# Split steps of a gate's weights respaced, the last norm factor's transfers on GpSimd's queue, and an activation table loaded at another place

## The chip, the cores and the metric

The kernel runs on 1 core of a Trainium2 chip. The metric is the device time of one execution in microseconds. The core's engines are TensorE (PE), VectorE (DVE), ScalarE (ACT), GpSimd (POOL) and SyncE (SP, which here only issues DMAs). They run apart from each other, each through its own instructions in order, and wait for one another by semaphores.

## The reference

One encoder layer on 1024 tokens of width 1024 (float32). Cut to what matters here:

```python
u = x @ w_in                                   # rq, rk, rv, rg, aq, ak, av
y_ret = bidirectional_retention(rq, rk, rv)    # 8 heads, chunks of 128
y_ret = group_norm(y_ret) * gn_gain * silu(rg) # (y - mu) * rsqrt(var + eps)
y_att = windowed_gqa(aq, ak, av, sink)         # 8 query heads, 2 kv heads
mix = concat(y_ret, y_att) @ w_out
h = layer_norm(alpha * x + mix)
ffn = (silu(h @ w_ffn_gate) * (h @ w_ffn_up)) @ w_ffn_down
ple = p @ w_ple_proj
h = layer_norm(alpha * h + ffn + sigmoid(h @ w_ple_gate) * ple)
```

## The kernel before

The order of every engine is that in which the kernel's Python calls its operations (a manual schedule). The large products run on TensorE in three passes (lines L77 to L79 and L803 to L805): each float32 operand is split into a rounded part and the rest, by a copy on ScalarE (L71) and a subtraction on VectorE (L72), and the passes are high by high, high by low and low by high. Many of the products are also put together in Strassen's manner, from seven block products instead of eight.

The layer goes by stages. First come the mixers: four pairs of heads (NPAIR = 4), each with its projections, retention and attention. Then the product with w_out, the first norm, the product of the per-layer gate (w_ple_gate, with a sigmoid), the gate and up products of the feed-forward part (the units of the list gunits, with silu), the product down, and the second norm.

Retention of a pair: `bt<-rv,qq` and `bt<-rv,pt` are TensorE's products L428, whose right sides qq and pt VectorE makes at L411; L490 and L491 do the like for the pair before. The norm of a pair's y is taken in two halves, hh = 0 and 1. TensorE sums the squares, VectorE makes a row of variances (L500), and then five steps follow, put off by the ticks of LAGS: `spread` (L505, the row into a tile sn of 128 x 8 by way of DMAs), `power` (L508, the power -1/2 on GpSimd), `store` (L511, sn into rnd in DRAM, 4 KB), `fetch` (L515, two DMAs that bring rnd back into a tile spread over 64 partitions each, 128 KB each; the tile is called kv for hh = 0 and rb for hh = 1), and `scaled` (L519, y times the gain times that tile, on VectorE). The last pair's second half (self.i = 3, hh = 1) is the last factor that the product with w_out waits for.

Beside the mixers' own work runs what later stages need, given as a list of (tick, step) pairs. `presplit_gate` makes the blocks of the per-layer gate's weights: for each of four k it loads two blocks of 512 KB (L653, at the times of load(k)) and then does seven steps. A step adds up to one sum on VectorE (L663, or none) and one `put`: a copy on ScalarE (L602), a subtraction on VectorE (L603, out<-in names pro<-pre,pro) and a store of 512 KB on SP (L604, pgd<-pro). The steps use two tiles pro in turn, so a step's copy waits for the store of the step before the last. The tick of each step is in the list `at`; one tick is a little over a microsecond of the mixers' time. With load(3) and an empty step there are 30 entries.

An instruction on ScalarE may need an activation table that is not loaded. A table load is then placed ahead of it (ACT_TABLE_LOAD). The tiny activation at L1854 has no other use than to have silu's table loaded; L1388 is the first silu that computes something, L1097 are the sigmoids, and L1424 and L1426 bring results of the units out of PSUM.

Of the kernel before, what the change touches and what calls it, by code (L numbers as in the profile page):

```python
# [11 lines left out]
AF = mybir.ActivationFunctionType  # L12
# [10 lines left out]
NPAIR = 4  # L23
# [19 lines left out]
def layer(tc, xT, xn, w_first, w_mt, w_rv, w_out, w_pg, w_pe, pT, w_gu, w_dn,  # L43
          consts, dec_b, dec_c, sink, gng, lnp, out):
    nc = tc.nc
    act, dve, pool, pe, sp = nc.scalar, nc.vector, nc.gpsimd, nc.tensor, nc.sync
# [12 lines left out]
    def nm(s):  # L59
        uid[0] += 1  # L60
        return f"{s}{uid[0]}"
# [19 lines left out]
    def behind(ins):  # L81

        tc.add_manual_dep(ins.ins, recent[0], mybir.DependencyInfo(
            mybir.DependencyClass.NoSync, mybir.DependencyReason.DATA), reason="order")
        return ins
# [35 lines left out]
    def a_tile(shape, name, tag=None, dt=F32):  # L121

        turnA[0] += tag is None
        return big.tile(list(shape), dt, tag=tag or f"A{turnA[0] % 2}", bufs=4, name=nm(name))
# [8 lines left out]
    def bt(shape, tag, bufs=None, dt=F32):  # L133
        return bpool.tile(list(shape), dt, tag=tag, bufs=bufs, name=nm(tag))
# [15 lines left out]
    with tc.manual_schedule(engines={mybir.EngineType.DVE, mybir.EngineType.SP}):  # L150
        for kt in range(KT):
            r = xraw[kt]
# [240 lines left out]
    class Retention:  # L393
# [100 lines left out]
        def norm(self, hh):  # L494

            b = self.o.rearrange("p n c -> p (n c)")
            for k in range(2):
                pe.matmul(b, ones, self.sq[k], start=k == 0, stop=k == 1)
            row = bt([2, HF], "kv0")
            behind(dve.tensor_scalar(row, b[0:2], 1.0 / 64, EPS, ALU.mult, ALU.add))  # L500
            sm, r, home = bt([P, 2, 8], "sn", 1), bt([P, HF], ("kv1", "rb")[hh]), rnd[2 * self.i + hh]

            def spread():
                for h in range(2):
                    sp.dma_start(sm[64 * h:64 * h + 64, 0], row[h:h + 1].rearrange("o (q e) -> o q e", e=8))  # L505

            def power():
                behind(pool.tensor_tensor(sm[:, 1], sm[:, 0], cst[:, C_MH:C_MH + 1].to_broadcast([P, 8]), ALU.pow))  # L508

            def store():  # L510
                sp.dma_start(home, sm[:, 1])  # L511

            def fetch():
                for h in range(2):
                    sp.dma_start(r[64 * h:64 * h + 64], home[64 * h:64 * h + 64].rearrange("q e -> (q e)").partition_broadcast(64))  # L515

            def scaled():
                y = self.half(hh)
                behind(dve.scalar_tensor_tensor(y, y, gn[:, self.i:self.i + 1], r, ALU.mult, ALU.mult))  # L519

            later.extend((ticks[0] + at, f) for at, f in zip(LAGS, (spread, power, store, fetch, scaled)))
# [79 lines left out]
    def put(x, o, dst):  # L601
        behind(act.activation(o[:, 0, :], x, AF.Copy))  # L602
        behind(dve.tensor_tensor(o[:, 1, :], x, o[:, 0, :].bitcast(F32), ALU.subtract))  # L603
        sp.dma_start(dst, o.bitcast(F32))  # L604
# [40 lines left out]
    def presplit_gate():  # L645

        first, other = ([a_tile([P, 2, HF], "pre", t) for _ in range(2)] for t in ("A1", "A0"))
        ops = [a_tile([P, 2, HF], "pro", "A1", F32R) for _ in range(2)]
        n = [0]

        def load(k):
            for j in range(2):
                sp.dma_start((other if k == 1 else first)[j], w_pg[j, k])  # L653

        def steps(k):
            raw = other if k == 1 else first

            (a11, a21), (a12, a22) = ([raw[j][:, i, :] for i in range(2)] for j in range(2))

            def s(p, x, *sums):  # L660
                def f():
                    for a in sums:
                        behind(dve.tensor_tensor(*a))  # L663
                    put(x, ops[n[0] % 2], pgd[p - 1, k])
                    n[0] += 1
                return f

            return [s(1, a11), s(4, a22), s(2, a12), s(5, a22, (a22, a21, a22, ALU.add)),
                    s(7, a21, (a21, a11, a21, ALU.subtract)), s(6, a11, (a11, a22, a11, ALU.subtract)),
                    s(3, a12, (a12, a12, a11, ALU.subtract))]  # L670

        load(0)
        load(1)
        k0, k1, k2, k3 = map(steps, range(4))
        k1[0] = pair_of(k1[0], lambda: load(2))
        k3[0:0] = [lambda: load(3), lambda: None]
        at = [2 + 3.4 * k for k in range(12)] + [55 + 2.5 * k for k in range(2)] + [65 + 1.9 * k for k in range(7)] + \
            [78.5 + 2 * k for k in range(9)]
        return [(ticks[0] + t, f) for t, f in zip(at, k0 + k1 + k2 + k3, strict=True)]

    def pair_of(f, g):
        def both():
            f()
            g()
        return both
# [4 lines left out]
    def ytile(k):  # L690
        if ys[k] is None:
            ys[k] = a_tile([P, S], "y", "A0" if k < 4 else "A1")
        return ys[k]
# [46 lines left out]
    with tc.manual_schedule(engines={mybir.EngineType.PE}):  # L740
# [17 lines left out]
        r = Retention(0, y0, states)  # L758
# [6 lines left out]
        for i in range(1, NPAIR):  # L765
            assert i == 1 or not side, len(side)
            r = Retention(i, ytile(2 * i), states)
# [419 lines left out]
    frights, fsum = {}, []  # L1187
# [305 lines left out]
    for n in range(NP):  # L1493
        for u in plan(n):
            k = len(gunits)
# [51 lines left out]
    def op_arena(t, n=4):  # L1547
        arena("op", t, n)
# [249 lines left out]
    def ahead_g(k, upto):  # L1798

        def finish():  # L1800
            while urgent:
                urgent.pop(0)()

        units = [g[3] for g in gunits] + [2.72]
        room = units[k + 1] - gunits[k][4] - debt[0] if k >= 0 else 100.0
        while items and items[0].unit < upto and items[0].slots <= len(oslots) and (items[0].us <= room or items[0].unit <= k + 1):
            room -= items[0].us
            items.pop(0).issue()
            finish()
        finish()  # L1810
        if held and held[0][0].unit <= k + 1:
            release()
        debt[0] = max(-0.6, -room)
# [25 lines left out]
    with tc.manual_schedule(engines={ET.PE, ET.DVE, ET.Activation, ET.Pool, ET.SP}):  # L1839
        for _ in range(4):  # L1840
            oslots.append(wp.tile([P, 2, HF], F32R, tag="w", bufs=4, name=nm("w")))
            oslots.append(ct([P, 2, HF], "u", 4, F32R))
        sums2.extend(a_tile([P, 2, HF], "sums") for _ in range(2))
        fa = big16((P, 4, 2, 2, Q))
        halves4 = [(fa[:, k, 0], fa[:, k, 1]) for k in range(4)]
        halves4.append(tuple(ct([P, 2, Q], "sg", 2, F32R) for _ in range(2)))
        fsum.extend([cst[:, 0:Q], cst[:, Q:2 * Q], *(ct([P, Q], "fs", 2) for _ in range(2))])
        fwide = ct([P, 2, Q], "p", 2)
        fine, more = fine_right(2, halves4[:3]), fine_right(4, halves4[3:])
        fine += more  # L1850
        homes.update((name, a_tile([P, 2, HF], "ev")) for name in ("spare", "s1", "u2", "c11", "u3", "c22"))
        FINE4 = len(plan(0)) + len(plan(1)) - 2
        FINES = (2, 4, 7, 9, 20, 23, 26, FINE4)
        act.activation(fsum[3][:, 0:1], fsum[0][:, 0:1], AF.Silu)  # L1854
        ahead_g(-1, 4)
        for k in range(NG):
            gunits[k][1]()
            gunits[k][2]()
            if k in FINES:
                at = max([-1] + [i for i, x in enumerate(items) if x.right]) + 1  # L1860
                for x in fine.pop(0):
                    at += 1
                    x.unit, x.right = items[at].unit, True
                    items.insert(at, x)
                    at += 1
            ahead_g(k, k + 1 + min(9, 4 + k))
            while stores and stores[0][0] <= k:
                stores.pop(0)[1]()
            j = k + 1 - NG
            if j == -6:  # L1870
                while items:
                    items.pop(0).issue()
                release()
                arenas_a()
                op_arena(ct([P, 4, 2, HF], "h0a", dt=F32R))
                arena("chain", ct([P, 8, HF], "h0b"), 8)
            if j == -4:
                for _ in range(3):
                    op_arena(big16((P, 4, 2, HF)))
            if j >= -6:  # L1880
                ahead(0, j + 7)
            if j >= -4:
                ahead(1, j + 5)
        arena("b", big.tile([P, 8, HF], F32, tag="H", bufs=4, name=nm("H")), 8)
        arena("chain", ct([P, 8, HF], "h2"), 8)
        op_arena(ct([P, 4, 2, HF], "h3", dt=F32R), 4)
        rings["op"] += [ct([P, 2, HF], "u", 4, F32R) for _ in range(2)]
        for k in range(ND):
            d_step(k)
# [83 lines left out]
```

## Time and profile before

| | us |
|---|---|
| median of 3 runs | 1171.9 |
| lowest, highest run | 1169.49, 1171.92 |
| the profiled execution's own time | 1172.7 |
| its span in the trace | 1170.6 |
| TensorE busy in it | 1156.5 |
| VectorE, ScalarE, GpSimd busy | 900.4, 580.1, 121.0 |

Times in the trace count from the span's start. A row of a timeline has the start, the duration, the engine, the line, the operation and its tiles, and in square brackets the idle time before it and what ended that. A row of a table of waits has the engine and its line, what it waited for, the sum of the waits, their number and the longest. A row of the DMA view has the destination and source, the issuing queue, the number, the size of one and the median time from issue to landing. The granted clock of TensorE was 0.998 of full speed.

### The profile page before, as it was taken

What the parts mean: (1) busy time and instruction counts of PE and PEld (TensorE: products, weight loads), DVE (VectorE), ACT (ScalarE), POOL (GpSimd) and SP (SyncE); (2) the same over time, 40 slices, a digit from 0 to 9 for tenths busy, and PEclk for the clock granted to TensorE, in tenths of its full rate; (3) what the DMA queues carried; (4) which work ended last, traced back from release to release, by engine and by line L of the source; (5) the groups of instructions that cost most, each with busy time, mean ns of one, the idle gap of its engine ahead of it and who ended that gap; (6) DMA issues with size and microseconds to landing.
All of it is one profiled execution on the core that took longest, in us unless ns stands there. A gap on an engine that the chain in (4) does not pass through costs nothing.

```text
span 1170.6 us, 17933 instructions
## 1 busy us (share of the span) xinstructions
PE 1156.5 (99%) x6330; PEld 971.5 (83%) x6330; DVE 900.4 (77%) x1746; ACT 580.1 (50%) x1181; POOL 121.0 (10%) x181
## 2 busy tenths in 40 slices
PE   9999999999999999999999999999999999999996
PEld 7888888788887888888888888888888888888885
DVE  4666688777869688947998988888888976773677
ACT  5566348686756256214445434443344445552463
POOL 2001021202010021000000000000000020133232
PEclk9999999999999999999999999999999999999999
DMA  6345665746356955665322222232223289999977
GB/s 252 100 153 207 246 207 193 244 159 223 127 190 230 365 172 196 261 195 201 117 90 105 112 105 100 102 135 101 99 72 136 89 249 349 350 225 203 261 173 216
DMA packets 84378, 213.86 MB, mean 183 GB/s; under 512 B 12225, under 2 KB 17473, under 8 KB 84289
## 3 DMA queue, kind: packets, MB, share of 16 engines
q1 hardware_dynamic: 75648, 195.94, 47.6%
q0 software_dynamic: 8640, 16.78, 8.2%
q8 instruction: 50, 0.82, 0.3%
q14 instruction: 40, 0.32, 0.1%
HBM read 141.32 MB, written 62.16 MB: 174 GB/s over the span
## 4 chain that ended last, share of the span: by engine, by line
PE 86%; DVE 6%; DMA 4%; ACT 2%; issue 1%; POOL 0%; SPq 0%; DVEq 0%; ACTq 0%; POOLq 0%
PE bmm L803 8%; PE bmm L804 8%; PE bmm L805 7%; PE bt L803 6%; PE bt L804 6%; PE bt L805 6%; PE bmm L77 4%; PE bs L803 4%; PE bs L805 4%; PE bs L804 4%; PE bmm L79 4%; PE bmm L78 4%; PE bo L805 3%; PE bo L803 3%; PE bo L804 3%
## 5 line engine op out<-in xcount | busy, mean ns | idle before, releaser
L77 PE MATMUL bmm<-H,w 128*128 128x512 f32 x240 | 97.3, 405 | 0.0
L78 PE MATMUL bmm<-H,w 128*128 128x512 f32 x240 | 93.9, 391 | 0.0
L79 PE MATMUL bmm<-H,w 128*128 128x512 f32 x240 | 93.9, 391 | 0.0
L1388 ACT ACTIVATE ev<-ev 128x512 f32<-128x512 f32 x42 | 26.5, 630 | 104.3 <-DVE ev L1417 92.8
L1562 POOL DMA_DIRECT2D h0b<-in_w_dn x24 | 21.6, 899 | 540.7 <-DVE ev L1368 504.9
L77 PEld LDWEIGHTS bmm<-H,w 128*128 128x128 f32 x240 | 45.1, 188 | 11.1 <-issue 1.4
L79 PEld LDWEIGHTS bmm<-H,w 128*128 128x128 f32 x240 | 45.1, 188 | 10.3
L78 PEld LDWEIGHTS bmm<-H,w 128*128 128x128 f32 x240 | 45.2, 188 | 7.9
L554 ACT ACTIVATE sc<-sc,st 128x385 f32<-128x385 f32 (+1 forms) x64 | 37.2, 585 | 15.6 <-DVE st L552 15.3
L550 DVE CUSTOM_DVE_ANT_0 sc<-cst,bs,skb 128x384 f32<-128x384 f32 (+1 forms) x64 | 35.0, 575 | 8.3 <-PE bs L549 7.8
L1417 DVE TENSOR_TENSOR ev<-ev,bt 128x512 f32<-128x512 f32 x44 | 30.1, 683 | 12.5 <-PE bt L805 12.5
L1368 DVE TENSOR_TENSOR ev<-ev,bs 128x256 f32<-128x256 f32 x63 | 25.6, 418 | 15.5 <-PE bs L805 14.7
L1390 DVE TENSOR_TENSOR ev<-ev 128x512 f32<-128x512 f32 x42 | 29.0, 691 | 10.5 <-ACT ev L1388 9.0
L803 PE MATMUL bmm<-H,u 128*128 128x512 f32 x92 | 36.2, 393 | 0.2 <-ACT ev L1426 0.2
L804 PE MATMUL bmm<-H,u 128*128 128x512 f32 x92 | 36.0, 392 | 0.0
L805 PE MATMUL bmm<-H,u 128*128 128x512 f32 x92 | 35.8, 389 | 0.0
L72 DVE TENSOR_TENSOR w<-raw,w 128x512 fp32r<-128x512 f32 x34 | 23.1, 688 | 16.2 <-ACT w L71 16.1
L545 POOL COPY sc<-skb 128x1 f32<-128x1 f32 x64 | 15.6, 253 | 188.9 <-PE bt L572 144.5
L560 ACT ACTIVATE sc<-sc,st 128x384 f32<-128x384 f32 (+1 forms) x64 | 34.2, 580 | 1.2 <-DVE st L558 0.9
L71 ACT ACTIVATE H<-ln 128x512 fp32r<-128x512 f32 (+1 forms) x34 | 22.7, 675 | 21.2 <-DVE ln L1052 7.2
L803 PE MATMUL bmm<-H,w 128*128 128x512 f32 x84 | 32.9, 392 | 0.0
L804 PE MATMUL bmm<-H,w 128*128 128x512 f32 x84 | 32.9, 392 | 0.0
(802 smaller groups left out, 3898.4 us busy)
## 6 DMA issues: line engine op xcount, KB each, us to landing
ad<-ev SPq DMA_DIRECT2D x33, 512.0 KB, 2.6
pgd<-pro SPq DMA_DIRECT2D x28, 512.0 KB, 3.0
raw<-in_w_gu SPq DMA_DIRECT2D x22, 512.0 KB, 3.6
ln<-in_w_gu SPq DMA_DIRECT2D x22, 512.0 KB, 3.9
raw<-ad SPq DMA_DIRECT2D x40, 256.0 KB, 5.6
ln<-ad SPq DMA_DIRECT2D x37, 256.0 KB, 6.0
H<-in_w_dn SPq DMA_DIRECT2D x33, 256.0 KB, 7.4
wod<-aq SPq DMA_DIRECT2D x15, 512.0 KB, 2.8
```

The costliest lines, as they stand in the source:

```text
L77: pe.matmul(o, lh, rh, start=start, stop=False)
L78: pe.matmul(o, lh, rl, start=False, stop=False)
L79: recent[0] = pe.matmul(o, ll, rh, start=False, stop=stop).ins.name
L550: dve.tensor_tensor_reduce(sc[g][:, :nk], cst[:, tc0:tc0 + nk], b[:, :nk], slope(i, g), skb[:, 2 * i + g:2 * i + g + 1], ALU.add, ALU.max, ...
L554: act.activation(sc[g][:, :nk + 1], sc[g][:, :nk + 1], AF.Exp, bias=st_[:, 1, j, g:g + 1], accum_out=st_[:, 2, j, g:g + 1])
L560: behind(act.activation(sc[g][:, :nk], sc[g][:, :nk], AF.Copy, scale=st_[:, 3, j, g:g + 1]))
L803: pe.matmul(o, lh, rh, start=start, stop=False, skip_group_check=True)
L804: pe.matmul(o, lh, rl, start=False, stop=False, skip_group_check=True)
L805: pe.matmul(o, ll, rh, start=False, stop=stop, skip_group_check=True)
L1388: act.activation(c[:, 0, :], c[:, 0, :], AF.Silu)
L1390: dve.tensor_tensor(c[:, 1, :], c[:, 0, :], c[:, 1, :], ALU.mult)
L1417: dve.tensor_tensor(get(name), ev[left][:, m, :], right, ALU.add)
```

## The change

Three things are changed. In `presplit_gate` the list of ticks is spread otherwise: 14 entries from tick 2 in steps of 2.8, then 7 from tick 60 and 9 from tick 73 in steps of 1.9. Before there were 12 from tick 2 in steps of 3.4, 2 from 55, 7 from 65 and 9 from 78.5. In `norm` the store and the fetch of the last pair's second half are issued by GpSimd (pool) in place of SP. And the tiny silu activation is called behind the first unit of the gate in place of ahead of all units.

```diff
--- before.py
+++ after.py
@@ -500,6 +500,8 @@
             behind(dve.tensor_scalar(row, b[0:2], 1.0 / 64, EPS, ALU.mult, ALU.add))
             sm, r, home = bt([P, 2, 8], "sn", 1), bt([P, HF], ("kv1", "rb")[hh]), rnd[2 * self.i + hh]
 
+            q = pool if hh and self.i == NPAIR - 1 else sp
+
             def spread():
                 for h in range(2):
                     sp.dma_start(sm[64 * h:64 * h + 64, 0], row[h:h + 1].rearrange("o (q e) -> o q e", e=8))
@@ -508,11 +510,11 @@
                 behind(pool.tensor_tensor(sm[:, 1], sm[:, 0], cst[:, C_MH:C_MH + 1].to_broadcast([P, 8]), ALU.pow))
 
             def store():
-                sp.dma_start(home, sm[:, 1])
+                q.dma_start(home, sm[:, 1])
 
             def fetch():
                 for h in range(2):
-                    sp.dma_start(r[64 * h:64 * h + 64], home[64 * h:64 * h + 64].rearrange("q e -> (q e)").partition_broadcast(64))
+                    q.dma_start(r[64 * h:64 * h + 64], home[64 * h:64 * h + 64].rearrange("q e -> (q e)").partition_broadcast(64))
 
             def scaled():
                 y = self.half(hh)
@@ -674,8 +676,7 @@
         k0, k1, k2, k3 = map(steps, range(4))
         k1[0] = pair_of(k1[0], lambda: load(2))
         k3[0:0] = [lambda: load(3), lambda: None]
-        at = [2 + 3.4 * k for k in range(12)] + [55 + 2.5 * k for k in range(2)] + [65 + 1.9 * k for k in range(7)] + \
-            [78.5 + 2 * k for k in range(9)]
+        at = [2 + 2.8 * k for k in range(14)] + [60 + 1.9 * k for k in range(7)] + [73 + 1.9 * k for k in range(9)]
         return [(ticks[0] + t, f) for t, f in zip(at, k0 + k1 + k2 + k3, strict=True)]
 
     def pair_of(f, g):
@@ -1851,7 +1852,6 @@
         homes.update((name, a_tile([P, 2, HF], "ev")) for name in ("spare", "s1", "u2", "c11", "u3", "c22"))
         FINE4 = len(plan(0)) + len(plan(1)) - 2
         FINES = (2, 4, 7, 9, 20, 23, 26, FINE4)
-        act.activation(fsum[3][:, 0:1], fsum[0][:, 0:1], AF.Silu)
         ahead_g(-1, 4)
         for k in range(NG):
             gunits[k][1]()
@@ -1864,6 +1864,8 @@
                     items.insert(at, x)
                     at += 1
             ahead_g(k, k + 1 + min(9, 4 + k))
+            if k == 0:
+                act.activation(fsum[3][:, 0:1], fsum[0][:, 0:1], AF.Silu)
             while stores and stores[0][0] <= k:
                 stores.pop(0)[1]()
             j = k + 1 - NG
```

TensorE's order is the same in both. The lines of after are two higher than those of before from L503 on, one higher from L679 to L1853, and again two from L1867 on. The numbers in the names below are those of buffers.

VectorE, from the last split steps of pair 1's stage up to pair 2's pt; pre and pro are the gate's blocks. Before:

```order
L603 TENSOR_TENSOR pro_1168<-pre_1163,pro_1168 128x512
L663 TENSOR_TENSOR pre_1164<-pre_1164,pre_1163 128x512
L519 SCALAR_TENSOR_TENSOR y_1596<-y_1596,gn,kv_2110 128x512
L251 SCALAR_TENSOR_TENSOR aq_2236<-bmm_2242,aq_2236 64x512
L411 TENSOR_TENSOR qq_2330<-bt_2325,kd 128x512
L603 TENSOR_TENSOR pro_1167<-pre_1163,pro_1167 128x512
L251 SCALAR_TENSOR_TENSOR aq_2237<-bmm_2242,aq_2237 64x512
L411 TENSOR_TENSOR qq_2330<-bt_2325,kd 128x512
L603 TENSOR_TENSOR pro_1168<-pre_1164,pro_1168 128x512
L72 TENSOR_TENSOR w_2335<-raw_2333,w_2335 128x512
L72 TENSOR_TENSOR w_2338<-raw_2333,w_2338 128x512
L411 TENSOR_TENSOR pt_2360<-bt_2355,kd 128x512 x2
```

After:

```order
L665 TENSOR_TENSOR pre_1164<-pre_1164,pre_1163 128x512
L251 SCALAR_TENSOR_TENSOR aq_2249<-bmm_2125,aq_2249 64x512
L605 TENSOR_TENSOR pro_1168<-pre_1164,pro_1168 128x512
L500 TENSOR_SCALAR kv_2288<-bo_2201 2x512
L72 TENSOR_TENSOR w_2335<-raw_2333,w_2335 128x512
L521 SCALAR_TENSOR_TENSOR y_1604<-y_1604,gn,kv_2116 128x512
L411 TENSOR_TENSOR qq_2330<-bt_2325,kd 128x512
L251 SCALAR_TENSOR_TENSOR aq_2248<-bmm_2254,aq_2248 64x512
L411 TENSOR_TENSOR qq_2330<-bt_2325,kd 128x512
L72 TENSOR_TENSOR w_2338<-raw_2333,w_2338 128x512
L251 SCALAR_TENSOR_TENSOR aq_2249<-bmm_2254,aq_2249 64x512
L411 TENSOR_TENSOR pt_2360<-bt_2355,kd 128x512 x2
```

In before two L603 and two L72 stand between the first qq (L411) and pt, and L663 and L603 right up to the norm L519. In after all the L605 and L665 (before's L603 and L663) lie ahead of L521 (before's L519), and the last of them ahead of L500.

SP's queue at the last factor; sn is the factor as made on GpSimd, u and w are loads for the product with w_out. Before:

```order
L604 DMA ped<-aq_3046 128x1024
L505 DMA sn_3719<-kv_3717 64x1x8 x2
L511 DMA rnd<-sn_3719 128x8
L604 DMA ped<-aq_3046 128x1024
L515 DMA rb_3720<-rnd 64x512 x2
L814 DMA u_3835<-wod 128x1024
L814 DMA w_3837<-wod 128x1024
L814 DMA u_3839<-wod 128x1024
```

After:

```order
L606 DMA ped<-aq_3046 128x1024
L507 DMA sn_3719<-kv_3717 64x1x8 x2
L606 DMA ped<-aq_3046 128x1024
L815 DMA u_3835<-wod 128x1024
L815 DMA w_3837<-wod 128x1024
L815 DMA u_3839<-wod 128x1024
```

GpSimd's queue at the same place, after:

```order
L547 COPY sc_3606<-skb 128x1
L510 TENSOR_TENSOR sn_3564<-sn_3564,cst 128x8
L510 TENSOR_TENSOR sn_3719<-sn_3719,cst 128x8
L513 DMA rnd<-sn_3719 128x8
L517 DMA rb_3720<-rnd 64x512 x2
L915 TENSOR_TENSOR stt_3930<-stt_3930,cst 128x1
```

VectorE behind it, where L519 (L521 in after) takes the factor and H are splits for the product with w_out. Before:

```order
L723 SCALAR_TENSOR_TENSOR sq_3788<-sq_3788,bmm_3761 128x512
L724 SCALAR_TENSOR_TENSOR y_2323<-sq_3788,y_2323 128x512
L519 SCALAR_TENSOR_TENSOR y_2323<-y_2323,gn,rb_3720 128x512
L72 TENSOR_TENSOR H_3849<-y_1162,H_3849 128x512
L72 TENSOR_TENSOR H_3849<-y_468,H_3849 128x512
L72 TENSOR_TENSOR H_3849<-y_1596,H_3849 128x512
```

After:

```order
L605 TENSOR_TENSOR aq_3046<-rk_3047,aq_3046 128x512
L724 SCALAR_TENSOR_TENSOR sq_3788<-sq_3788,bmm_3761 128x512
L725 SCALAR_TENSOR_TENSOR y_2323<-sq_3788,y_2323 128x512
L72 TENSOR_TENSOR H_3849<-y_1162,H_3849 128x512
L521 SCALAR_TENSOR_TENSOR y_2323<-y_2323,gn,rb_3720 128x512
L72 TENSOR_TENSOR H_3849<-y_468,H_3849 128x512
```

The store and the two fetches have left SP's queue and stand on GpSimd's behind the power, and the first split H ahead of the scaling by the factor.

ScalarE at the first gate unit. Before:

```order
L1097 ACTIVATE sg_5328<-H_4563 128x512
L1424 ACTIVATE ev_5354<-bmm_5368 128x512
L1252 ACTIVATE w_5342<-sums_5346 128x512
L1424 ACTIVATE ev_5354<-bmm_5386 128x512
L1252 ACTIVATE u_5343<-sums_5347 128x512
L1388 ACT_TABLE_LOAD
L1388 ACTIVATE ev_5358<-ev_5358 128x512
```

After:

```order
L1098 ACTIVATE sg_5328<-H_4563 128x512
L1425 ACTIVATE ev_5354<-bmm_5367 128x512
L1253 ACTIVATE w_5342<-sums_5346 128x512
L1868 ACT_TABLE_LOAD
L1868 ACTIVATE fs_5352<-cst 128x1
L1425 ACTIVATE ev_5354<-bmm_5386 128x512
L1253 ACTIVATE u_5343<-sums_5347 128x512
```

The table load stands two operations earlier, ahead of the second eviction L1425 (before's L1424). The load that before makes at L1854, in the product with w_out, is not in after's order.

## The prediction

> **What bounds the kernel now.** I read the busy shares first, then TensorE's waits, then the timelines around the few waits that the change touches.
>
> ```profile
> PE 1156.5 (99%) x6330; PEld 971.5 (83%) x6330; DVE 900.4 (77%) x1746; ACT 580.1 (50%) x1181; POOL 121.0 (10%) x181
> PE bt L428 <- DVE pt L411: 2.0, 1, 2.0
> PE bo L142 <- POOL sq L139: 1.3, 1, 1.3
> PE bs L803 <- ACT h0b L972: 0.6, 1, 0.6
> PE bt L803 <- DMA u<-wod: 0.4, 1, 0.4
> PE bt L77 <- DMA p<-ptd: 0.3, 1, 0.3
> PE bt L572 <- ACT ptr L574: 0.3, 1, 0.3
> PE bmm L803 <- ACT ev L1426: 0.2, 1, 0.2
> ```
>
> TensorE is busy 1156.5 of 1170.6 us and all that it waits for by the profile comes to about 5 us. TensorE's order does not change, so no more than these waits can be gained, and whatever is made late elsewhere must appear here as a new one. The largest, 2.0 us, lies where retention pair 1 gives way to pair 2. What is won or lost before the end of the mixers stays won or lost: TensorE has no idle time afterwards in which to catch up.
>
> **Part 1, the split steps.** VectorE ahead of that wait, and TensorE at it:
>
> ```profile
> 216.80 0.98 DVE L491 TENSOR_TENSOR rb<-qq,pt 128x512 fp32r<-128x512 f32 x1
> ...
> 219.13 0.69 DVE L663 TENSOR_TENSOR pre<-pre,pre 128x512 f32<-128x512 f32 x1
> ...
> 223.59 0.69 DVE L603 TENSOR_TENSOR pro<-pre,pro 128x512 fp32r<-128x512 f32 x1 [0.40 <-ACT pro L602]
> 224.19 0.68 DVE L663 TENSOR_TENSOR pre<-pre,pre 128x512 f32<-128x512 f32 x1
> ...
> 228.92 0.68 DVE L603 TENSOR_TENSOR pro<-pre,pro 128x512 fp32r<-128x512 f32 x1
> ...
> 230.73 1.28 DVE L411 TENSOR_TENSOR pt<-bt,kd 128x512 f32<-128x512 f32 x2
> 229.16 1.03 PE L428 MATMUL bt<-rv,qq 128*64 128x64 f32 x28
> 232.16 1.04 PE L428 MATMUL bt<-rv,pt 128*64 128x64 f32 x28 [1.97 <-DVE pt L411]
> ```
>
> From L491 to the two pt of L411, VectorE has one gap, 0.40 us: it is simply full. In that stretch the order of before has 21 operations, that of after 15. The six that have gone are three L603 and three L663 of the gate's splits. Their starts follow one another by about 0.61 us (223.59 to 224.19), so pt comes some 3.6 us earlier, and TensorE needs it only 2.0 us earlier (229.16 + 1.03 for the first L428, so 230.2 in place of 232.16). The surplus of 1.6 us is the cover if something else there is late. Take −2.0. Bounds: 0 if another input holds pt, and no better than −2.0, since the first L428 runs straight on from TensorE's earlier work.
>
> The steps that leave go earlier, and two more of them fall in pair 0's stage:
>
> ```profile
> 168.62 1.29 DVE L411 TENSOR_TENSOR pt<-bt,kd 128x512 f32<-128x512 f32 x2
> 170.19 0.63 PE L428 MATMUL bt<-rv,pt 128*64 128x64 f32 x15
> 174.81 0.68 DVE L663 TENSOR_TENSOR pre<-pre,pre 128x512 f32<-128x512 f32 x1
> ...
> 176.54 0.69 DVE L603 TENSOR_TENSOR pro<-pre,pro 128x512 fp32r<-128x512 f32 x1
> 181.84 0.55 PE L572 MATMUL bt<-cst,sc 128*128 128x128 f32 x3 [0.28 <-ACT ptr L574]
> ```
>
> At the change from pair 0 to pair 1 one more L603 (0.61 us) stands before pt of L411, which ends at 169.91 for a TensorE that takes it at 170.19. With that margin of 0.28 the new wait is about 0.35. In return, between 174 and 181 two L663 and two L603 have gone (2.4 us), and the wait of 0.28 at 181.84 goes with them. The two cancel: 0. Bounds: −0.3 if the margin is larger, and +2.4 if all four VectorE operations of the two extra steps landed on TensorE. Each step's ScalarE copy and its store on SP move with it. ScalarE is busy half the time and SP has no waiting reader of these stores in the mixers. They cost nothing, unless a load of the weights delays a store and the store ScalarE's next copy.
>
> **Part 2, the last factor through GpSimd.** The chain of before, from SP, GpSimd and VectorE, and the DMA rows of that window:
>
> ```profile
> 345.38 1.64 POOL L508 TENSOR_TENSOR sn<-sn,cst 128x8 f32<-128x8 f32 x1 [12.16 <-DMA sn<-kv]
> 347.05 0.33 SPq L511 DMA_DIRECT2D rnd<-sn  x1
> ...
> 348.49 1.11 SPq L515 DMA_DIRECT2D rb<-rnd  x2
> 349.65 0.58 SPq L814 DMA_DIRECT2D u<-wod  x1
> 353.06 0.75 DVE L519 SCALAR_TENSOR_TENSOR y<-y,gn,rb 128x512 f32<-128x512 f32 x1 [1.62 <-DMA rb<-rnd]
> rb<-rnd SPq DMA_DIRECT2D x2, 128.0 KB, 3.7
> rnd<-sn SPq DMA_DIRECT2D x1, 4.0 KB, 1.4
> ```
>
> Power, store (1.4), fetch (3.7), then L519, with VectorE idle 1.62 us for it. From 353.06 on VectorE does not idle again until past TensorE's wait of 0.6 us:
>
> ```profile
> 371.19 0.68 DVE L876 TENSOR_TENSOR ln<-ln,y 128x512 f32<-128x512 f32 x1
> 371.90 0.63 ACT L71 ACTIVATE h0a<-ln 128x512 fp32r<-128x512 f32 x1 [1.78 <-DVE ln L876]
> 372.44 0.58 ACT L972 ACTIVATE h0b<-bs 128x512 f32<-128x512 f32 x1
> 373.07 0.50 PE L803 MATMUL bs<-w,H 128*128 128x512 f32 x1 [0.55 <-ACT h0b L972]
> ```
>
> L876 follows L519, ScalarE's L71 follows L876, the eviction L972 is queued behind that L71, and TensorE needs its bank. So a factor that lands X later moves TensorE by X here. In its favour, in after one split (L72, 0.60) runs ahead of L519, in the idle time, while ScalarE's first L972 comes behind one more L71: of the 0.60 I count 0.45. The cost is X − 0.45. What SP gains, loads of u and w issued up to 3 us earlier and the 0.4 us wait for u gone, is made up again by the wait at 373, which hangs on L519 alone, and is not counted. Behind the waiting fetch on GpSimd's queue nothing is due for a long while.
>
> X is not in the trace of before, where GpSimd issues nothing so early. The nearest rows:
>
> ```profile
> kv<-rnd SPq DMA_DIRECT2D x8, 128.0 KB, 3.2
> L1562 POOL DMA_DIRECT2D h<-in_w_dn x9 | 7.9, 880 | 9.0 <-issue 5.6 <-DVE H L72 2.8 <-DVE u L72 0.6
> acc<-R POOLq DMA_DIRECT2D x12, 256.0 KB, 5.4
> h<-in_w_dn POOLq DMA_DIRECT2D x1, 256.0 KB, 4.2
> ```
>
> An issue keeps GpSimd 0.88 us where SP took 0.33 for the store and 1.11 for both fetches. With the same travel times, X = (0.88 − 0.33) + (1.76 − 1.11) = 1.2. Low end: the issuing is hidden and the fetch, no longer behind SP's other transfers, takes the 3.2 us of its sisters in place of 3.7: X = −0.5. High end: 4.2 us, one of GpSimd's shortest, for the store and for the fetch: 2.8 + 0.5 + 0.65 = 3.95. By the median row of 5.4 it would be 4.0 + 1.7 + 0.65 = 6.35, but those 256 KB transfers run among full DMA engines. I take 1.2, nearest to the rows of the very same transfers: cost +0.75, from −0.95 to +3.5. The Trainium skill ("DMA: Bandwidth & Descriptors", section "SWDGE vs HWDGE vs iDMA" and the table of the page's head) speaks against the change: a queue served by GpSimd's software is the slower one, its first byte at about 1 us against 0.6 us. Taken on top of the issue times that would add an estimated 0.8 us for store and fetch, and the sum would come out 0.8 us higher.
>
> **Part 3, silu's table.**
>
> ```profile
> 362.84 1.28 ACT L1854 ACT_TABLE_LOAD   x1
> 544.82 0.63 ACT L1252 ACTIVATE w<-sums 128x512 fp32r<-128x512 f32 x1 [2.62 <-DVE sums L1288]
> 549.79 1.28 ACT L1388 ACT_TABLE_LOAD   x1 [2.41 <-DVE ev L1417]
> 558.09 0.50 PE L803 MATMUL bmm<-H,u 128*128 128x512 f32 x1 [0.20 <-ACT ev L1426]
> ```
>
> Before, the table is loaded at 362.84 and again at 549.79, in front of the first silu; after, once, behind L1252 of 544.82, where ScalarE stands idle for microseconds at a time. The 1.28 us leave the path from L1417 over L1388 to the products that VectorE and ScalarE owe TensorE at 558; its wait there is 0.20. Take −0.2 (0 if that wait hangs on other rows; a loss only if the load fell in front of an eviction, and the idle time there covers it).
>
> **Sum.** −2.0 + 0 + 0.75 − 0.2 = −1.45. The profiled execution took 1172.7 us, 0.8 above the median 1171.9 of the runs: 1171.25 for it, 1170.4 against the median. About 0.2%, or 2.3 us, is what a measurement of this kernel can tell from no change.
>
> **Rivals.**
> *A, the forecast:* the pt wait goes, the factor comes 0.35 to 3.95 late: −2.3 to +1.3 us, 1169.6 to 1173.2. Chance 0.42.
>
> *B, GpSimd's way is no slower:* the issue is hidden and the fetch no longer waits behind SP's store of ped. For it: the DMA engines are nearly empty at 347, and the sisters' fetch takes 3.2. Against it: no GpSimd row below 4.2. X between −0.5 and 0.35 gives −2.0 − 0.2 + (−0.95 to −0.1): −3.15 to −2.3, so 1168.7 to 1169.6. Chance 0.38. The Trainium skill ("DMA: Bandwidth & Descriptors", section "Anatomy of one DMA — SWDGE (gpsimd) path") has a fit of 2.0 us plus bytes over 436e3 per microsecond for such a transfer: as an estimate 2.0 for the store and 2.3 for a fetch, which with one issue between them would set the factor 0.7 earlier than before and the total at −3.35.
>
> *C, slower:* GpSimd's transfers behave as its later ones do. The earlier loads of u and w, 512 KB each, now fill the DMA engines just when the small transfers need them; store and fetch each take the 5.4 of the median row. X = 6.35 costs 5.9, the total is +3.7: 1175.6. It decides from X = 4.95 on (+2.3). Against it: those rows move 256 KB, the store 4 KB. Chance 0.15.
>
> *D, the steps only move the wait:* the two extra steps of pair 0's stage cost TensorE their four VectorE operations, 2.4 us. The gain at 232 is paid back, and the total is +0.95: 1172.9; with a factor over 2.55 late as well it passes +2.3. Against it: the freed 2.4 us behind them. Chance 0.05, of it 0.03 beyond +2.3.
>
> **Chances and range.** Faster by over 0.2%: B, 0.38. Within: A and 0.02 of D, 0.44. Slower: C and 0.03 of D, 0.18. The range takes in all of A, B to just past its end and the nearer part of C (X up to 4.95 and somewhat beyond): 1168.5 to 1174.4.
>
> **What would show it.** Right: no wait of L428 on L411 at about 230; a wait of a few tenths near 170; L519 starting 0.35 to 4 us later than before, counted from the end of the power, and the wait on L972 longer or shorter with it; five table loads in place of six. Wrong: a wait for pt, or one of a microsecond between 140 and 182 (D), L519 no later than before by that count (B) or some 5 us later (C).

## The result, and the profile after

The changed kernel takes 1178.45 us in the median of its runs against 1170.7 for the kernel before: ratio 1.0065, 95% interval [1.0043, 1.0087], so it is slower by some 7.6 us (5 to 10). The forecast was 1170.4, that is 1.45 under the median then known, 1171.9, with a range up to 1174.4. The profiled execution took 1179.2 us, its span 1176.9 against 1170.6.

TensorE's waits in the changed kernel (engine and line, what it waited for, sum, number, longest):

```profile
PE bt L806 <- DVE H L72: 7.1, 1, 7.1
PE bo L142 <- POOL sq L139: 1.3, 1, 1.3
PE bs L550 <- DVE pt L461: 1.0, 1, 1.0
PE bt L574 <- ACT ptr L576: 0.4, 1, 0.4
```

The wait of 2.0 us on pt of L411 is gone. One of 7.1 us has come, in front of the product with w_out, and one of 1.0 us on another pt, that of L461. The queues that lead to the first, in the order SP, GpSimd, VectorE (L521 is before's L519):

```profile
346.08 0.33 SPq L606 DMA_DIRECT2D ped<-aq  x1
346.76 0.32 SPq L815 DMA_DIRECT2D u<-wod  x1
347.18 0.47 SPq L815 DMA_DIRECT2D w<-wod  x1
347.71 0.49 SPq L815 DMA_DIRECT2D u<-wod  x1
...
345.10 1.63 POOL L510 TENSOR_TENSOR sn<-sn,cst 128x8 f32<-128x8 f32 x1 [12.49 <-DMA sn<-kv]
347.07 0.79 POOL L513 DMA_DIRECT2D rnd<-sn  x1 [0.33 <-POOL sn L510]
353.84 1.06 POOL L517 DMA_DIRECT2D rb<-rnd  x2 [5.99 <-issue]
...
360.96 0.75 DVE L521 SCALAR_TENSOR_TENSOR y<-y,gn,rb 128x512 f32<-128x512 f32 x1 [9.54 <-DMA rb<-rnd]
rb<-rnd POOLq DMA_DIRECT2D x2, 128.0 KB, 5.9
rnd<-sn POOLq DMA_DIRECT2D x1, 4.0 KB, 6.2
```

From the power's end (346.73) to L521 it is 14.2 us, against 6.04 before (347.02 to 353.06). The store of 4 KB landed after 6.2 us in place of 1.4, the fetch after 5.9 in place of 3.7. SP, no longer held up by the factor, issued its loads of u and w at 346.76 to 347.71, in before only from 349.65 on. The factor's transfers now run beside them.

Part 1's place, TensorE and then VectorE:

```profile
229.76 0.99 PE L428 MATMUL bt<-rv,pt 128*64 128x64 f32 x28
...
235.10 0.44 PE L550 MATMUL bs<-k,aq 128*128 128x384 f32 x1 [0.99 <-DVE pt L461]
...
223.68 0.75 DVE L521 SCALAR_TENSOR_TENSOR y<-y,gn,kv 128x512 f32<-128x512 f32 x1 [1.31 <-DMA kv<-rnd]
...
227.80 1.29 DVE L411 TENSOR_TENSOR pt<-bt,kd 128x512 f32<-128x512 f32 x2
...
231.31 0.17 DVE L560 RECIPROCAL st<-st 128x2 f32<-128x2 f32 x1 [1.22 <-ACT sc L556]
231.77 0.42 DVE L436 COPY kv<-bt 128x256 f32<-128x256 f32 x1 [0.29 <-issue]
...
234.36 1.28 DVE L461 TENSOR_TENSOR pt<-bs,dt 128x512 f32<-128x512 f32 x2
```

L428 starts without a wait. Half of the gain comes back 5 us later: VectorE stands 1.22 us at L560, which waits for ScalarE's exponentials, and pt of L461 is queued behind it.

And the clock, after the long wait (stretch, its length, busy time of TensorE, its weight loads, VectorE, ScalarE, GpSimd, then the granted clock, the DMA engines' busy share and GB/s):

```profile
350.00:355.00 5.00, 5.00 (x24) 4.00 (x22) 1.39 (x3) 4.93 (x10) 1.06 (x2) 1.00 0.96 348
355.00:360.00 5.00, 0.24 (x2) 0.00 (x0) 0.00 (x0) 1.39 (x3) 0.00 (x0) 0.77 1.00 324
360.00:365.00 5.00, 2.63 (x6) 2.15 (x7) 4.04 (x7) 0.00 (x0) 0.00 (x0) 0.50 0.07 25
365.00:370.00 5.00, 5.00 (x17) 3.93 (x16) 5.00 (x9) 2.24 (x4) 0.00 (x0) 0.70 0.00 0
```

Where the time went, by the starts of the same matmul in both traces (the order of TensorE is the same, so the n-th of the one is the n-th of the other, counted from 0):

| matmul | before | after | after − before |
|---|---|---|---|
| L584, pair 2 (1564th) | 247.11 | 246.24 | −0.87 |
| behind the long wait (2389th) | 355.77 | 362.37 | +6.60 |
| 44 matmuls later (2433rd) | 366.78 | 375.29 | +8.51 |
| feed-forward (3600th) | 621.35 | 627.47 | +6.12 |

Part 1 brought under 1 us and the factor cost 7.3 to 7.5. The lower clock and the order behind it cost another 1.9: while the clock was halved the lag grew by 2.1, the wait of before at 357 gave 0.35 of that back, and 0.2 came just ahead of the 2433rd. Behind that 2.4 came back, most of it where before waits at 373 (0.7), 527 (0.5) and 558 (0.4).

### The profile page after: what moved, and what is told of

It reads as the page before. It is cut to its first block, busy times and chain, and to the rows that moved or that the text cites. A ratio compares the mean times of both kernels' runs of the same rounds, so it can differ in the third digit from the quotient of the medians.

```text
span 1176.9 us, 17929 instructions
## 1 busy us (share of the span) xinstructions
PE 1157.9 (98%) x6330; PEld 974.1 (83%) x6330; DVE 902.3 (77%) x1746; ACT 578.5 (49%) x1180; POOL 121.9 (10%) x184
## 4 chain that ended last, share of the span: by engine, by line
PE 95%; DMA 2%; DVE 1%; ACT 1%; issue 0%; SPq 0%; DVEq 0%; POOL 0%; ACTq 0%
PE bmm L804 8%; PE bmm L805 8%; PE bmm L806 8%; PE bt L806 6%; PE bt L804 6%; PE bt L805 6%; PE bmm L77 6%; PE bmm L78 5%; PE bmm L79 5%; PE bs L806 4%; PE bs L805 4%; PE bs L804 4%; PE bo L806 4%; PE bo L805 4%; PE bo L804 4%; PE bo L586 2%
## 5 line engine op out<-in xcount | busy, mean ns | idle before, releaser
L77 PE MATMUL bmm<-H,w 128*128 128x512 f32 x240 | 97.3, 405 | 0.2 <-ACT H L71 0.2
L78 PE MATMUL bmm<-H,w 128*128 128x512 f32 x240 | 94.0, 392 | 0.0
L79 PE MATMUL bmm<-H,w 128*128 128x512 f32 x240 | 93.9, 391 | 0.0
L72 DVE TENSOR_TENSOR w<-raw,w 128x512 fp32r<-128x512 f32 x34 | 23.1, 688 | 16.7 <-ACT w L71 16.6
L576 ACT ACTIVATE ptr<-bt 128x384 f32<-128x384 f32 (+1 forms) x64 | 26.5, 457 | 13.2 <-PE bt L574 13.1
L804 PE MATMUL bmm<-H,w 128*128 128x512 f32 x84 | 32.9, 392 | 0.0
```

The lines of the kernel that those rows point to most:

```text
L77: pe.matmul(o, lh, rh, start=start, stop=False)
L78: pe.matmul(o, lh, rl, start=False, stop=False)
L79: recent[0] = pe.matmul(o, ll, rh, start=False, stop=stop).ins.name
L576: act.activation(p_[:, :hi - lo, :], tb[:, :hi - lo, :], AF.Copy)
L804: pe.matmul(o, lh, rh, start=start, stop=False, skip_group_check=True)
```

## Experiments

My theory after the result: the factor's transfers were slow because the loads of u and w, let loose by the same edit, fill the DMA engines. Rival: GpSimd's queue is slow by itself, or in its first use.

**Parts 1 and 3 alone (e1).**

```diff
-            q = pool if hh and self.i == NPAIR - 1 else sp
+            q = sp
```

> The changed kernel with store and fetch of the last factor back on SP (parts 1 and 3 alone). Theory: the whole loss hangs on GpSimd's transfers, so the wait of 7.1 us for H behind L521 is gone, the trace has the new wait of about 1 us on pt of L461 near 235, and the time is 0.5 to 1.5 us under the kernel before. Rival, that the respaced steps themselves cost time: at or above the kernel before.

Ratio to the kernel before 0.9995, interval [0.9985, 1.0006]. The long wait is gone, so the loss is part 2's; the rest is not told from no change. Its waits:

```profile
PE bt L804 <- ACT h0b L973: 1.5, 1, 1.5
PE bo L142 <- POOL sq L139: 1.3, 1, 1.3
PE bs L550 <- DVE pt L461: 1.1, 1, 1.1
```

The first of them, at 366 for an eviction by ScalarE, is a second place where a gain is lost: by the starts of the same matmuls this trace is 2.25 us ahead of before in front of it and 0.58 behind it, and 0.7 comes back where before waits at 373.

**Part 2 alone (e2)**, in the kernel before:

```diff
+            q = pool if hh and self.i == NPAIR - 1 else sp
...
-                sp.dma_start(home, sm[:, 1])
+                q.dma_start(home, sm[:, 1])
...
-                    sp.dma_start(r[64 * h:64 * h + 64], ...)
+                    q.dma_start(r[64 * h:64 * h + 64], ...)
```

> The kernel before with only store and fetch of the last factor on GpSimd. Theory: the scaling by the factor starts some 14 us after the power's end in place of 6, and the time is 7 to 8.5 us over the kernel before. Rival, that parts 1 and 2 work against each other only together: under 4 us over it.

GpSimd and VectorE:

```profile
345.00 1.64 POOL L510 TENSOR_TENSOR sn<-sn,cst 128x8 f32<-128x8 f32 x1 [12.21 <-DMA sn<-kv]
...
360.84 0.75 DVE L521 SCALAR_TENSOR_TENSOR y<-y,gn,rb 128x512 f32<-128x512 f32 x1 [9.16 <-DMA rb<-rnd]
```

Ratio 1.0067, [1.0049, 1.0085]. The whole loss is there without parts 1 and 3, as expected; the power ends at 346.64 and the scaling starts at 360.84, 14.2 us later.

**Part 1 alone (e3) and part 3 alone (e4)**, each in the kernel before:

```diff
-        at = [2 + 3.4 * k for k in range(12)] + [55 + 2.5 * k for k in range(2)] + [65 + 1.9 * k for k in range(7)] + \
-            [78.5 + 2 * k for k in range(9)]
+        at = [2 + 2.8 * k for k in range(14)] + [60 + 1.9 * k for k in range(7)] + [73 + 1.9 * k for k in range(9)]
```

```diff
-        act.activation(fsum[3][:, 0:1], fsum[0][:, 0:1], AF.Silu)
...
+            if k == 0:
+                act.activation(fsum[3][:, 0:1], fsum[0][:, 0:1], AF.Silu)
```

> The kernel before with only the new list of ticks. Theory: the wait of 2.0 us on pt of L411 near 232 goes, about 1 us of it comes back as a wait on pt of L461 near 235, and a few tenths near 207; net 0.5 to 1 us under the kernel before. Rival (my forecast's sum): 2 us under it.

> The kernel before with only the silu activation behind the gate's first unit. Theory: one table load fewer, the wait of 0.2 us near 558 gone, and 1.5 us of ScalarE's time gone at 363; 0 to 0.6 us under the kernel before. Rival: the load delays an eviction and adds a wait near 545.

e3: 0.9997 [0.9987, 1.0007]; e4: 1.0003 [0.9991, 1.0014]. Neither can be told from no change; both intervals hold what I expected and also nothing at all, but e3's (1.5 us at most) excludes the 2.0 us of my sum. In e3's trace the wait of 2.0 us is gone and the new one on pt of L461 measures 0.7 us. In e4's the wait of 0.2 us at 558 is gone, but so it is in e2 and e3, which load the table as before does.

**Loads held behind the factor (e5).** GpSimd still carries store and fetch, but SP's queue first waits for the fetched tile (rnd is two rows larger in this run and the next, not shown here):

```diff
                     q.dma_start(r[64 * h:64 * h + 64], ...)
+                if q is pool:
+                    sp.dma_start(rnd[8], r[:, 0:8])
```

> The changed kernel, but SP must first read eight columns of the fetched tile back to DRAM before it issues the loads of u and w, so that these come behind the factor. It tells contention from a slow queue. Contention (the loads of u and w fill the DMA engines while the small transfers wait): the store lands within 2.5 us and the scaling starts 6 to 8 us after the power's end. Slow queue (GpSimd's transfers need this long by themselves): the store still takes over 5 us and the scaling starts 12 us or more after it. In both cases TensorE then waits for u, so the total is no verdict.

GpSimd's rows, VectorE's and the DMA view's:

```profile
344.42 1.63 POOL L510 TENSOR_TENSOR sn<-sn,cst 128x8 f32<-128x8 f32 x1 [12.19 <-DMA sn<-kv]
346.38 0.79 POOL L513 DMA_DIRECT2D rnd<-sn  x1 [0.33 <-POOL sn L510]
...
352.86 0.75 DVE L523 SCALAR_TENSOR_TENSOR y<-y,gn,rb 128x512 f32<-128x512 f32 x1 [1.86 <-DMA rb<-rnd]
rb<-rnd POOLq DMA_DIRECT2D x2, 128.0 KB, 2.8
rnd<-sn POOLq DMA_DIRECT2D x1, 4.0 KB, 2.5
```

With the loads out of the way, the same transfers on the same queue take 2.5 and 2.8 us, and the scaling starts 6.8 us after the power's end in place of 14.2. The DMA engines are 0.34 busy from 346 to 350 and 0.18 from 349 to 353, where in the changed kernel they are 0.67, 0.96 and 1.00 in the three stretches of 5 us from 345. So it is contention with the loads; whether the small transfers lose the time in the DMA engines or at the memory, no run separates. What is left for GpSimd's queue itself is 0.8 us against the 6.04 of before, 0.6 against the 6.24 of e1. (TensorE then waits 3.5 us for u; the one run took 1174.84. e6 and e8 are single runs as well.)

**First use (e6).** One more store of 4 KB on GpSimd's queue, 14 us earlier.

```diff
+                if self.i == NPAIR - 1 and not hh:
+                    pool.dma_start(rnd[9], sm[:, 1])
```

> The changed kernel with one more store of 4 KB on GpSimd's queue, to a place that nobody reads, behind the power of the first half some 14 us earlier, when the DMA engines are about 0.6 full. If the first use of the queue is what costs, the extra store takes over 5 us and the real one about 2.5 us. If contention costs, the extra one takes 2 to 4 us and the real one again about 6 us.

The extra store, the first use of this queue, and then the real one:

```profile
rnd<-sn POOLq DMA_DIRECT2D x1, 4.0 KB, 2.6
...
rnd<-sn POOLq DMA_DIRECT2D x1, 4.0 KB, 5.7
```

The first use took 2.6 us among DMA engines half full, the second 5.7 among the loads. First use is not the cause. (The run took 1178.8 us.)

**ScalarE's queue (e7).**

```diff
-            q = pool if hh and self.i == NPAIR - 1 else sp
+            q = act if hh and self.i == NPAIR - 1 else sp
```

> The changed kernel with ScalarE's queue in place of GpSimd's for store and fetch; SP's loads of u and w go out early as in the changed kernel. Contention: store and fetch are as slow as on GpSimd, the scaling starts 12 us or more after the power's end, and the time is 5 us or more over the kernel before. Slow queue of GpSimd: the store lands in 1.4 to 2.5 us, the scaling starts 6 to 7.5 us after the power's end, and the time is that of parts 1 and 3 alone, within 1 us.

```profile
rb<-rnd ACTq DMA_DIRECT2D x2, 128.0 KB, 6.0
rnd<-sn ACTq DMA_DIRECT2D x1, 4.0 KB, 4.8
...
PE bt L806 <- DVE H L72: 5.1, 1, 5.1
```

Ratio 1.0038, [1.0023, 1.0052]. A queue that GpSimd has no part in is slow as well, 12.0 us from the power's end to the scaling (345.39 to 357.41), though a little less so than GpSimd's: the loss is some 4.5 us, just short of the 5 that I expected. Both queues beside SP's that were tried let the loads go first.

**Only the store on GpSimd (e8)**, the fetch on SP, where it stands ahead of the loads again.

```diff
-                    q.dma_start(r[64 * h:64 * h + 64], ...)
+                    sp.dma_start(r[64 * h:64 * h + 64], ...)
```

> The changed kernel with only the store on GpSimd; the fetch is on SP again, where the loads of u and w are behind it. Contention: with nothing but one store of 512 KB in flight the store on GpSimd lands in 2 to 3 us, and the scaling starts 7 to 8 us after the power's end. Slow queue: the store takes over 5 us, the scaling starts about 10 us after it.

```profile
rnd<-sn POOLq DMA_DIRECT2D x1, 4.0 KB, 2.5
...
353.31 0.75 DVE L521 SCALAR_TENSOR_TENSOR y<-y,gn,rb 128x512 f32<-128x512 f32 x1 [3.56 <-DMA rb<-rnd]
```

2.5 us for the store, the scaling 7.8 us after the power's end (345.49); the one run took 1173.0 us. This is what contention would give.

**The wait given back (e9).** Parts 1 and 3, and the softmax's reciprocal that held up pt of L461 put behind it:

```diff
-            later.append((ticks[0] + LAG, scaled))
+            later.append((ticks[0] + LAG + (1 if (i, n) == (2, 0) else 0), scaled))
```

> Parts 1 and 3 with the reciprocal of pair 2's first softmax block one tick later, which puts it (and ScalarE's scaling behind it) after pt of L461 on VectorE; TensorE's order of products is kept. It tests what gave the gain at 232 back. If VectorE's wait of 1.2 us for ScalarE's exponentials held pt of L461, the wait of 1.1 us on it near 235 falls to 0.3 or less and the time is about 0.8 us under parts 1 and 3. Rival, that TensorE's own product or ScalarE's copies of kv hold pt: the wait stays near 1 us.

VectorE there, and all waits of TensorE:

```profile
231.60 1.28 DVE L461 TENSOR_TENSOR pt<-bs,dt 128x512 f32<-128x512 f32 x2
232.80 0.15 DVE L560 RECIPROCAL st<-st 128x2 f32<-128x2 f32 x1
...
PE bo L142 <- POOL sq L139: 1.3, 1, 1.3
PE bt L804 <- ACT h0b L973: 1.1, 1, 1.1
PE bmm L77 <- ACT H L71: 0.4, 1, 0.4
```

The wait on pt of L461 is gone, and the ratio is 0.9974, [0.9965, 0.9984]: 3 us under the kernel before. That is more than the 0.8 us that I expected below e1; the two were timed beside different runs of before, so their difference has no interval. By the starts of the same matmuls e9's trace gains 1.3 us on e1's at pt of L461 and 0.4 at the wait on h0b. What had given part 1's gain back near 235 was VectorE's stand at L560.

**Another order on SP (e10), and both (e11).** Parts 1 and 3 with the last small presplit moved; e11 has this edit and that of e9:

```diff
-                side.extend(presplit_small(2, op, 27) + presplit_small(3, op, 34, rkx, ...))
+                side.extend(presplit_small(2, op, 27) + presplit_small(3, op, 37, rkx, ...))
```

> Parts 1 and 3 with the last step of the small presplit three ticks later in the list, by which its store of 512 KB (ped) stands ahead of the factor's store on SP and no longer between store and fetch; the factor stays on SP. If what the small transfers need is empty DMA engines and not another queue, the fetch takes some 3.2 us in place of 3.7 to 4.3, the scaling starts 5 to 5.5 us after the power's end in place of 6.25, and TensorE gains 0.5 to 1 us over parts 1 and 3. Rival, that ped ahead of the store holds the store back: the scaling starts later than 6.25 us after the power's end.

> Both of these together with parts 1 and 3, the version that the runs point to: 1.5 to 2 us under parts 1 and 3, so 2 to 3 us under the kernel before. If the gains meet another chain of waits at the product with w_out, under 1 us below parts 1 and 3.

e10: 0.9973, [0.9962, 0.9984]. The gain came, but not by my reason. SP, GpSimd and VectorE:

```profile
338.63 1.13 SPq L507 DMA_DIRECT2D sn<-kv  x2
339.81 0.58 SPq L815 DMA_DIRECT2D w<-wod  x1
...
343.82 0.32 SPq L513 DMA_DIRECT2D rnd<-sn  x1
346.67 1.10 SPq L517 DMA_DIRECT2D rb<-rnd  x2
...
341.06 1.64 POOL L510 TENSOR_TENSOR sn<-sn,cst 128x8 f32<-128x8 f32 x1 [9.19 <-DMA sn<-kv]
350.68 0.75 DVE L521 SCALAR_TENSOR_TENSOR y<-y,gn,rb 128x512 f32<-128x512 f32 x1
```

The store, now right behind ped, waited 2.85 us for its landing, and the scaling starts 8.0 us after the power's end, as the rival said. But the edit also put the spread of the variances (sn, L507) ahead of a load of w (in e1 that load, at 337.54, stands ahead of it): the power starts at 341.06, in e1 at 343.46, and L521 is still 0.7 us earlier and no longer waits for the factor. Which of the two, order of the spread or one split less behind L521, gave how much was not separated. The place is known: e10's trace ends 1.3 us ahead of e1's, and gains 1.6 at the wait of 1.5 on h0b, which is gone.

e11: 0.9965, [0.9952, 0.9978], 1167.65 us against 1171.93: the fastest version, some 4 us under the kernel before, where I expected 2 to 3. It is not told apart from e9 or e10 alone.

## Why the prediction was wrong

**The step that failed** is the one that priced X from GpSimd's and SP's rows and, apart from it, filed the loads of u and w as a gain "not counted". They were the cost. In before the order of SP's queue was a guard: a fetch that waits at its head keeps 1.5 MB of loads out of the DMA engines. The edit moved the fetch off that queue and took the guard away. X was not 1.2 but 8.2 (14.2 less 6.04). Without the loads the sum is near, 0.8 (e5), but that is in part luck: the second issue of the fetch, priced at 0.65, cost nothing (1.06 us for both on GpSimd, 1.11 on SP), the store took 1.1 more than on SP and the fetch 0.9 less, and GpSimd began the store 0.3 and the fetch 0.5 us later behind what each waits for than SP did. Rival C named the mechanism with a chance of 0.15 and priced it by the median of busy rows (X = 6.35); I argued it away by the store's 4 KB, but the store of 4 KB took 6.2 us, as long as the fetch of 128 KB.

The fit that the Trainium skill gives ("DMA: Bandwidth & Descriptors", section "Anatomy of one DMA — SWDGE (gpsimd) path") gave 2.0 and 2.3 us; with the loads held back (e5) they took 2.5 and 2.8, beside the loads 6.2 and 5.9. So here it holds within 0.5 us where little else moves and misses by about 4 us beside the loads. The later first byte that the prediction cites from the Trainium skill, 0.4 us for each of two transfers, has the size of e5's 0.8 us; no run shows that it is the cause.

**Carried to TensorE.** Right: a late L519 moves TensorE by nearly as much, 7.3 to 7.5 us where X − 0.45 with the measured X gives 7.75. The place was not the wait on L972 at 373 but the split H itself (7.1 us, at 362). Missed: the wait is long enough to lower the clock, about 2 us more. And not all that is lost before the end of the mixers stays lost: 2.4 us came back between 369 and 558.

**Part 1:** the wait on L411 went, but the cover was some 0.5 us and not 1.6: pt came 2.9 us earlier (227.80 for 230.73) and not 3.6, as VectorE now stood 1.31 us for the fetched kv at L521, and L428 starts 2.4 us earlier. The bound "no better than −2.0" was right, but the next late chains were not looked for: VectorE's order behind pt had L560 in front of L436 to L461. Of the 2.0 us about 1.0 came back there and some tenths at the wait on ptr. In e1, with the factor on SP, the wait on h0b at 366 took another 1.7 us, of which 0.7 came back at 373. The few tenths forecast near 170 did not come and the wait of 0.28 at 181.84 went, so the 0 for the moved steps is right only as a sum. No wait in these stages is above a few tenths, so rival D did not happen.

**Part 3:** five table loads in place of six and no wait of 0.2 near 558 in after. But e2 and e3, with six loads, do not have that wait either, so nothing shows that its going is part 3's; the −0.2 is not shown, and too small for e4 to tell.

## What to carry to other kernels

Moving a small, urgent transfer to another queue also frees what stood behind it on the old one. Ask first what those transfers are and whether they meet the urgent one in the DMA engines: an in-order queue may be what keeps them apart. And when a full engine's wait is taken away, follow the order some microseconds on: the next instruction that waits for another engine may be where the gain stops, as L560 was here.

## What the runs showed of the hardware

A store of 4 KB took 1.4 us on SP (before) and 2.5 on GpSimd (e5) with the DMA engines 0.39 and 0.34 busy, 2.8 on SP right behind a store of 512 KB (e10), and 6.2 (GpSimd), 5.7 (GpSimd, queue used before) and 4.8 (ScalarE) beside loads of 512 KB from another queue. The Trainium skill ("DMA: Bandwidth & Descriptors", section "SWDGE vs HWDGE vs iDMA") has each DMA engine take turns between its queues; no run here shows the turns, and a queue of its own did not keep a small transfer short.

After TensorE's wait of 7.1 us its granted clock was 0.50 from 360 to 365 and 0.70 from 365 to 370; after e7's wait of 5.1 us it was 0.60 and 0.72 in the stretches from 355 and 360. After e5's wait of 3.5 us it was 0.94 and 0.72 in these stretches: it fell at 359 to 360 (0.71), with TensorE at work again since 357.87. The wait of 2.0 us in before left no mark (1.00 from 228 to 240). The Trainium skill ("TensorE: Matmul & The Clock Gate", section "Part 1: The HAM clock gate") has the clock halved after about 3.4 us without work; the traces agree, with a fall after 3.5 us of waiting and none after 2.0. In the changed kernel the half clock put about 2 us on top of the wait of 7.1.
